# Spreading the sample tokens' rows over all partitions: DRAM scratch in place of selector matmuls

## The chip, the core and the metric

One core of a Trainium2 chip runs the whole program. The metric is the device time in microseconds (us), the median of several runs; less is better. The engines that matter are TensorE (PE, matmuls and transposes, with its weight loads shown apart as PEld), VectorE (DVE), ScalarE (ACT), GpSimd (POOL), and SyncE (SP), which here does nothing but issue the DMAs, one after another in program order.

## What is computed

One layer of a hybrid decoder runs for 256 prompt tokens and for 8 sample tokens, one each of 8 sequences. Two pieces of it treat the sample tokens apart, because each of the 8 has a state or a cache of its own. Everything else is large projections over 264 token columns.

```python
# retention, per head: every sample token b has its own 128 x 128 state
new_state = state * chunk_decay + k^T v        # rank-one update of that token's state
out       = q . new_state
# cross-attention, per head of 512 channels: every sample token has its own 256 memory keys and values
s = einsum('bshd,bmhd->bhsm', q, mk) * 512 ** -0.5
p = softmax(s)
o = einsum('bhsm,bmhd->bshd', p, mv)
```

The outputs are the hidden rows of both groups, the memory keys and values of the prompt, the retention states of both groups, and one set of value rows of the sample tokens.

## The kernel before, in words

**The weight stream.** All projections are one stream of 524 chunks, a chunk being 256 x 512 weights in fp32 (512 KB). SP loads a chunk (`emit_dma`, L1024), ACT rounds it to fp32r (`wh`, L1030), DVE takes the remainder (`wl`, L1038), and PE multiplies: 24 matmuls, three per 128 x 128 piece (L152 to L154), each over 264 columns. A loop at L1066 walks through the chunks. For chunk i it emits the remainder `wl` of chunk i + 2, the DMA of chunk i + 6, and then the 24 matmuls of chunk i, in four points of six. There are 5 raw buffers and 4 for the split halves, so each engine can run only some chunks ahead of PE. Every engine executes its own instructions strictly in the order in which they were emitted.

**Deferred work.** At each of the four points of a chunk `run_point` (L210) advances the small work: every due chain, and then one step of the first due task. A task is a Python generator; `yield 5` means: go on in five points at the earliest. So the small work is laid between the weight matmuls, and its place is decided by counting points, not by time. `flush` (L228) advances the point counter with no weight matmul in between until no chain, task or store is left.

**Retention of the sample tokens** (L568, eight heads, chunks 24 to about 75). The k and q columns of a head's 8 sample tokens are transposed to rows (L584), split into two fp32r halves in the tile `kq` (rows 0 to 7 and 32 to 39), and for each token b a matmul with a selector column of `sel`, broadcast to 128 columns, puts the sum of the two halves of row b on all 128 partitions, in the PSUM tile `bc` (L618). DVE then updates that token's state (L621) and multiplies it with the q row (L624, the sum lands in `rs_t`). Two tokens make one step, and a step is followed by `yield 2`.

**Cross-attention of the sample tokens** (`sample_attn`, L806, four heads in one lane, one after another). The q columns are transposed in four pieces (L810), split into `qs`, and for each token one selector matmul over 512 columns puts its q row on all partitions (`qb`, L819). DVE multiplies it with the token's keys (`kjk`, L822); the keys and later the values come as tiles `kv` of 512 KB with three buffers (`kv_fill`, L748, L752). The 16 columns of scores are transposed (L828), `softmax` (L790) works on 8 rows of 256, the probabilities are split into `pst`, and a selector matmul over 256 columns per token puts them on all partitions (`pb`, L842). DVE multiplies them with the values in four pieces per token (`vjk`, L845). At the end `join_o` (L785) writes the 8 sample columns of the head's output pair `oh`, `ol` next to the prompt's 256.

**Where the order ties these together.** The projection w_co starts at chunk 224 (`n_mem`) and reads the pairs `oh`, `ol` of head 0 in its chunks 224 and 225, of head 1 in 226 and 227, of head 2 in 228 and 229, and of head 3 from chunk 230 on. At chunk 230 (L1080) the loop calls `flush`, so that all work of the cross-attention is emitted ahead of the matmuls of chunk 230.

Of the kernel before, what the change touches and what calls it, by code (L numbers as in the profile page):

```python
# [30 lines left out]
def build(tc, I, O):  # L31
# [5 lines left out]
    with cst as cst, wpool as wpool, spool as spool, tpool as tpool, psum as psum:  # L37
        with tc.manual_schedule():
            _emit(tc, cst, wpool, spool, tpool, psum, I, O)


def _emit(tc, cst, wpool, spool, tpool, psum, I, O):
# [41 lines left out]
    sel = cst.tile([128, 8], F32R, name="sel")  # L84
# [115 lines left out]
    def store(dst, src, delay=10):  # L200
        stores.append((now[0] + delay, dst, src))
# [8 lines left out]
    def run_point():  # L210
# [13 lines left out]
        while stores and stores[0][0] <= now[0]:  # L224
            _, dst, src = stores.popleft()
            sp.dma_start(out=dst, in_=src)
# [131 lines left out]
    def clear():  # L358
        zt = half("zt")
        dve.memset(zt[:], 0.0)  # L360
        S["kq"] = [S["rpool"].tile([128, 256], F32R, name="kq", tag="kq", bufs=2) for _ in range(2)]
        yield
        for i in range(2):
            act.copy(S["kq"][i][:], zt[:, 0:256])
        dve.tensor_tensor(out=sel[:], in0=ident[:, 0:8], in1=ident[:, 32:40], op=ALU.add)
        act.activation(halfgn[:], gcol[:, G_GN:G_GN + 8], AF.Copy, scale=0.5)
# [179 lines left out]
    def ev_v(g):  # L546
        def ev(ps):
# [4 lines left out]
            if g == 0:  # L552
                S["state"] = {}
                load_state(0)
                load_state(1)
            for h in range(4 * g, 4 * g + 4):
                defer(retention(h), 3 + 16 * (h % 2), lane=f"r{h % 2}")
# [9 lines left out]

    def retention(h):  # L568
# [9 lines left out]
        kq = S["kq"][h % 2]  # L578
        tp = misc([128, 512], "tp")
# [3 lines left out]
        for i, src in enumerate((kt, qt)):  # L583
            transpose(tp[0:8, 256 + i * 128:384 + i * 128], src[:, 0:8])  # L584
# [3 lines left out]
        act.copy(kq[0:8, :], tp[0:8, 256:512])  # L588
        dve.tensor_tensor(out=kq[32:40, :], in0=tp[0:8, 256:512], in1=kq[0:8, :].bitcast(F32), op=ALU.subtract)
# [22 lines left out]
        yield  # L612
        rs_t = S["rpool"].tile([128, 8], F32, name="rs_t", tag="rs_t", bufs=2)
        for b0 in range(0, 8, 2):
            bc = misc([128, 2, 256], "bc")
            for j in range(2):
                b = b0 + j
                pe.matmul(bc[:, j, :], lhsT=sel[:, b:b + 1].broadcast_to([128, 128]), rhs=kq[:], start=True, stop=True)  # L618
            for j in range(2):
# [3 lines left out]
                j2 = S["rpool"].tile([128, 128], F32, name="rjk", tag="rjk", bufs=1)  # L623
                dve.scalar_tensor_tensor(out=j2[:], in0=st[:, b, :], scalar=1.0, in1=bc[:, j, 128:256],  # L624
                                         op0=ALU.mult, op1=ALU.mult, accum_out=rs_t[:, b:b + 1])
            yield 2
# [129 lines left out]
    def ev_cq(h):  # L756
        def ev(ps):
            if h == 0:
                zt = half("zt")
                dve.memset(zt[:], 0.0)  # L760
                S["qs"] = S["mpool"].tile([128, 512], F32R, name="qs", tag="qs", bufs=1)
                S["pst"] = S["mpool"].tile([128, 256], F32R, name="pst", tag="pst", bufs=1)
                act.copy(S["qs"][:], zt[:])
                act.copy(S["pst"][:], zt[:, 0:256])
# [40 lines left out]

    def sample_attn(h):  # L806
# [403 lines left out]
```

## Time and profile before

| | before |
|---|---|
| time, median of 3 runs | 1607.97 us (1607.68 to 1608.06) |
| span of the profiled execution, first to last instruction | 1605.7 us |
| time of the runs less that span | 2.3 us |
| PE busy | 1589.0 us, 99% |
| PE weight loads busy | 1560.8 us, 97% |
| DVE busy | 1049.4 us, 65% |
| ACT busy | 743.9 us, 46% |
| all DMA queues together | 326.15 MB, mean 203 GB/s |
| mean granted TensorE clock | 0.997 |

The page gives no time of the profiled execution other than its span. A busy PE row overlaps: matmuls are pipelined and a record of 284 ns starts about 120 ns after the one before it, so what a matmul costs PE is read from the distance between starts and not from its duration. Times of transfers are given from issue to landing.

### The profile page before, as it was taken

Reading aid. Unit: us, or ns where it says so; the run is one execution under the profiler, and the core shown is the slowest. Engines: PE = TensorE matmul, PEld = TensorE weight load, DVE = VectorE, ACT = ScalarE, POOL = GpSimd, SP = SyncE. Lnnn points to the kernel's source line nnn. Section 1 sums busy time; section 2 is a strip of 40 time slices with the busy share of each in tenths; the row PEclk is TensorE's granted clock in tenths of the full one; section 3 lists DMA queues with packets and bytes.
Section 4 is the critical chain, followed back from the end, with each engine's and each line's share of the span. In section 5 each row is a group of like instructions: output and inputs, shape, how many; then the busy total and the mean of one; then the engine's idle time right before and its main releaser. Section 6 shows DMA issues by size and latency. Waiting matters only on the chain.

```text
span 1605.7 us, 31031 instructions
## 1 busy us (share of the span) xinstructions
PE 1589.0 (99%) x12608; PEld 1560.8 (97%) x12608; DVE 1049.4 (65%) x1897; ACT 743.9 (46%) x1156; POOL 146.5 (9%) x138
## 2 busy tenths in 40 slices
PE   8999999999999999999999999999999999999997
PEld 7999999999999998999999999999999999999997
DVE  8758688678668777877655554554655555565555
ACT  5445466357444444444545443534444353444432
POOL 7403022010012111001000000000000000000000
PEclk9999999999999999999999999999999999999999
DMA  7565655455578887877555555455555555555552
GB/s 262 184 224 197 218 175 194 143 189 208 192 250 284 311 311 284 275 277 255 177 184 175 180 171 196 172 182 186 172 186 171 195 172 186 182 180 187 172 185 80
DMA packets 94222, 326.15 MB, mean 203 GB/s; under 512 B 10608, under 2 KB 15344, under 8 KB 94080
## 3 DMA queue, kind: packets, MB, share of 16 engines
q1 hardware_dynamic: 94080, 324.18, 59.2%
q8 instruction: 98, 1.61, 0.4%
q14 instruction: 44, 0.36, 0.1%
HBM read 313.03 MB, written 11.11 MB: 202 GB/s over the span
## 4 chain that ended last, share of the span: by engine, by line
PE 96%; DVE 2%; DMA 0%; issue 0%; ACT 0%; SPq 0%; POOL 0%; DVEq 0%; ACTq 0%
PE acc L152 28%; PE acc L153 28%; PE acc L154 28%; PE acc L176 2%; PE acc L178 2%; PE acc L177 2%; PE tp L96 1%; DVE wl L1038 1%; PE qb L819 0%; DMA hT<-in_xT_dram 0%; PE bc L618 0%; DVE xl L104 0%; PE spp L482 0%; DVE y L1121 0%; PE rsb L290 0%
## 5 line engine op out<-in xcount | busy, mean ns | idle before, releaser
L1030 ACT CAST wh<-w 128x1024 fp32r<-128x1024 f32 (+1 forms) x513 | 536.3, 1046 | 721.6 <-PE acc L153 638.7
L1038 DVE TENSOR_TENSOR wl<-w,wh 128x1024 fp32r<-128x1024 f32 (+1 forms) x513 | 631.2, 1243 | 255.1 <-ACT wh L1030 254.4
L152 PE MATMUL acc<-h2h,wh 128*128 128x264 f32 x1024 | 291.1, 284 | 0.0
L153 PE MATMUL acc<-h2l,wh 128*128 128x264 f32 x1024 | 291.0, 284 | 0.0
L154 PE MATMUL acc<-h2h,wl 128*128 128x264 f32 x1024 | 290.9, 284 | 0.0
L153 PE MATMUL acc<-rl,wh 128*128 128x264 f32 x992 | 282.3, 285 | 0.0
L154 PE MATMUL acc<-rh,wl 128*128 128x264 f32 x992 | 282.1, 284 | 0.0
L152 PE MATMUL acc<-rh,wh 128*128 128x264 f32 x992 | 282.1, 284 | 0.0
L152 PE MATMUL acc<-xh,wh 128*128 128x264 f32 x768 | 225.4, 293 | 0.2
L154 PE MATMUL acc<-xh,wl 128*128 128x264 f32 x768 | 219.9, 286 | 3.5 <-DVE wl L1038 2.9
L153 PE MATMUL acc<-xl,wh 128*128 128x264 f32 x768 | 219.6, 286 | 0.0
L152 PEld LDWEIGHTS acc<-h2h,wh 128*128 128x128 f32 x1024 | 192.9, 188 | 0.0
L153 PEld LDWEIGHTS acc<-h2l,wh 128*128 128x128 f32 x1024 | 192.8, 188 | 0.0
L154 PEld LDWEIGHTS acc<-h2h,wl 128*128 128x128 f32 x1024 | 192.6, 188 | 0.0
L152 PEld LDWEIGHTS acc<-rh,wh 128*128 128x128 f32 x992 | 187.0, 189 | 0.0
L153 PEld LDWEIGHTS acc<-rl,wh 128*128 128x128 f32 x992 | 186.8, 188 | 0.0
L154 PEld LDWEIGHTS acc<-rh,wl 128*128 128x128 f32 x992 | 186.5, 188 | 0.0
L154 PEld LDWEIGHTS acc<-xh,wl 128*128 128x128 f32 x768 | 145.7, 190 | 4.4 <-DVE wl L1038 3.7
L152 PEld LDWEIGHTS acc<-xh,wh 128*128 128x128 f32 x768 | 145.7, 190 | 1.9 <-ACT xh L103 0.7
L153 PEld LDWEIGHTS acc<-xl,wh 128*128 128x128 f32 x768 | 145.8, 190 | 0.2 <-DVE xl L104 0.2
L950 DVE TENSOR_TENSOR hT<-hT,acc 128x264 f32<-128x264 f32 x124 | 53.3, 430 | 73.4 <-PE acc L154 73.4
L92 POOL TENSOR_TENSOR msr<-msv,neghalf 128x3 f32<-128x3 f32 (+1 forms) x5 | 7.8, 1551 | 944.9 <-DVE msv L265 738.6
(255 smaller groups left out, 2800.0 us busy)
## 6 DMA issues: line engine op xcount, KB each, us to landing
w<-in_w_ff_dram SPq DMA_DIRECT2D x256, 512.0 KB, 4.1
w<-in_w_in_dram SPq DMA_DIRECT2D x95, 512.0 KB, 3.9
w<-in_w_out_dram SPq DMA_DIRECT2D x32, 512.0 KB, 4.1
w<-in_w_cq_dram SPq DMA_DIRECT2D x32, 512.0 KB, 4.2
kv<-in_kN_dram SPq DMA_DIRECT2D x32, 512.0 KB, 4.9
kv<-in_vT_dram SPq DMA_DIRECT2D x32, 512.0 KB, 5.2
w<-in_w_ck_dram SPq DMA_DIRECT2D x32, 512.0 KB, 5.3
w<-in_w_cv_dram SPq DMA_DIRECT2D x32, 512.0 KB, 4.4
```

The costliest lines, as they stand in the source:

```text
L92: gp.tensor_tensor(out=out, in0=in_, in1=neghalf[0:in_.shape[0], 0:n], op=ALU.pow)
L96: pe.transpose(out, in_, ident[0:p, 0:p])
L152: pe.matmul(ps, lhsT=a, rhs=xh, start=(i == 0), stop=False)
L153: pe.matmul(ps, lhsT=a, rhs=xl, start=False, stop=False)
L154: pe.matmul(ps, lhsT=b, rhs=xh, start=False, stop=(i == nk - 1))
L176: pe.matmul(ps, lhsT=a, rhs=hi[:, k, :], start=(kt == 0), stop=False)
L177: pe.matmul(ps, lhsT=a, rhs=lo[:, k, :], start=False, stop=False)
L178: pe.matmul(ps, lhsT=b, rhs=hi[:, k, :], start=False, stop=(kt == 15))
L950: dve.tensor_tensor(out=h[m], in0=h[m], in1=ps[m][:], op=ALU.add)
L1030: act.copy(hi[:, k, :], raws[i][:, k, :])
L1038: dve.tensor_tensor(out=lo[:, k, :], in0=raw[:, k, :], in1=hi[:, k, :].bitcast(F32), op=ALU.subtract)
```

## The change

The selector `sel`, the zeroed tiles `kq`, `qs` and `pst` and every matmul with `sel` are gone. Rows reach the partitions through DRAM instead: a small tile of rows is stored to a DRAM tile of the new pool `dpool`, and a DMA reads one row (or two) back with the same source for all 128 partitions.

- Retention: a new task `sample_rows(g)` gathers the k and q columns of four heads, transposes them in two pieces, copies them to a tile of 32 rows and stores it. Each step of two tokens reads its rows as a tile `bkq` of 128 x 512 (four buffers, asked for one step ahead). A step is followed by `yield 4` instead of `yield 2`, and the steps wait until the store has been emitted, then 6 points more.
- Cross-attention: the q columns are transposed in one piece and stored as `qd`; each token's row comes back as a tile `brow` of 128 x 512 (three buffers, two tokens ahead). The probabilities are stored as `pd` and come back as 128 x 256. Between the stages stand new waits of some points: 8, until the store was emitted, and 4 for the q rows; until the store was emitted, 4, and 4 for the probabilities.
- Stores are emitted when their own due time has come, no longer strictly first in, first out.

```diff
     def store(dst, src, delay=10):
-        stores.append((now[0] + delay, dst, src))
+        e = [now[0] + delay, dst, src, False]
+        stores.append(e)
+        return e
...
+    def sample_rows(g):
+        cols = S["rpool"].tile([128, 2, 32], F32, name="kqcol", tag="kqcol", bufs=1)
+        for i, w in enumerate("kq"):
+            act.copy(cols[:, i, :].rearrange("p (m b) -> p m b", m=4), S[w][g][:, :, 0:8])
+        yield 2
+        tp = misc([32, 2, 128], "tp")
+        for i in range(2):
+            transpose(tp[:, i, :], cols[:, i, :])
+        rows = S["rpool"].tile([32, 256], F32, name="kqrow", tag="kqrow", bufs=1)
+        act.copy(rows[:], tp[:].rearrange("p a d -> p (a d)"))
+        S["kqd"][g] = dpool.tile([32, 256], F32, name=f"kqd{g}")
+        S["kqe"][g] = store(S["kqd"][g][:], rows[:], 3)
+        yield
+
+    def rows_of(h, b0):
+        t = S["rpool"].tile([128, 2, 256], F32, name="bkq", tag="bkq", bufs=4)
+        r = 8 * (h % 4) + b0
+        sp.dma_start(out=t[:].rearrange("p b f -> p (b f)"),
+                     in_=S["kqd"][h // 4][r:r + 2, :].rearrange("b f -> (b f)").partition_broadcast(128))
+        return t
...
         for b0 in range(0, 8, 2):
-            bc = misc([128, 2, 256], "bc")
-            for j in range(2):
-                b = b0 + j
-                pe.matmul(bc[:, j, :], lhsT=sel[:, b:b + 1].broadcast_to([128, 128]), rhs=kq[:], start=True, stop=True)
+            bc = ahead
+            if b0 < 6:
+                ahead = rows_of(h, b0 + 2)
...
-            yield 2
+            yield 4
...
+    def spread_row(src):
+        t = S["mpool"].tile([128, 512], F32, name="brow", tag="brow", bufs=3)
+        n = src.shape[-1]
+        sp.dma_start(out=t[:, 0:n], in_=src.partition_broadcast(128))
+        return t
...
+        sc = small(16, "scs")
+        yield 8
+        while not e[3]:
+            yield 1
+        rows = deque(spread_row(qd[b].rearrange("m d -> (m d)")) for b in range(2))
+        yield 4
...
+            sent.append(store(pd[:], p[0:8, :], 2))
+            yield
+
+        sent = []
         softmax(tp[:], 8, spread_p)
         yield 11
+        while not sent or not sent[0][3]:
+            yield 1
+        yield 4
+        rows = deque(spread_row(pd[b]) for b in range(2))
+        yield 4
```

The order of the instructions moves with it. The first place is DVE around the values of head 3, the last head of the cross-attention. In the program before, its last groups of four products `vjk` stand between the remainders `wl` of the weight chunks, and `ol<-so` is the write of the head's sample columns:

```order
L793 TENSOR_SCALAR nb<-mx 128x1
L845 SCALAR_TENSOR_TENSOR vjk,so<-kv,pb 128x256 x4
L798 RECIPROCAL rc<-sm 128x1
L799 TENSOR_SCALAR ex<-ex,rc 128x256
L792 TENSOR_REDUCE mx<-sc 128x1
L793 TENSOR_SCALAR nb<-mx 128x1
L1038 TENSOR_TENSOR wl<-w,wh 128x1024
L798 RECIPROCAL rc<-sm 128x1
L799 TENSOR_SCALAR ex<-ex,rc 128x256
L1038 TENSOR_TENSOR wl<-w,wh 128x1024
L908 TENSOR_TENSOR pl<-tp,ph 128x256 x2
L101 TENSOR_TENSOR ol<-so,oh 128x4x8
```

In the changed program the same place on DVE reads as follows; `mx` to `ex` with 8 rows is the softmax of the sample tokens:

```order
L843 SCALAR_TENSOR_TENSOR kjk,scs<-kv,brow 128x512 x2
L1065 TENSOR_TENSOR wl<-w,wh 128x1024
L101 TENSOR_TENSOR ol<-op,oh 128x256 x2
L1065 TENSOR_TENSOR wl<-w,wh 128x1024
L801 TENSOR_REDUCE mx<-tp 8x1
L802 TENSOR_SCALAR nb<-mx 8x1
L807 RECIPROCAL rc<-sm 8x1
L808 TENSOR_SCALAR ex<-ex,rc 8x256
L872 SCALAR_TENSOR_TENSOR vjk,so<-kv,brow 128x256 x32
L101 TENSOR_TENSOR ol<-so,oh 128x4x8
L1065 TENSOR_TENSOR wl<-w,wh 128x1024 x2
```

All 32 products of head 3 now stand in one piece behind its softmax, with no remainder of a weight chunk among them. The second place is SP at the same point. Before, the last loads of values and the weight chunks of w_co take turns:

```order
L752 DMA kv<-in_vT_dram 128x1024
L1024 DMA w<-in_w_co_dram 128x1024
L752 DMA kv<-in_vT_dram 128x1024
L1024 DMA w<-in_w_co_dram 128x1024 x4
L226 DMA out_mem_v_dram<-vnat 128x1024
L1024 DMA w<-in_w_co_dram 128x1024 x23
```

In the changed program SP has, from the third load of values of head 3 on (`pd_8989` is the DRAM tile of head 3's probabilities):

```order
L767 DMA kv<-in_vT_dram 128x1024
L227 DMA pd_8989<-ex 8x256
L818 DMA brow<-pd_8989 128x256 x3
L767 DMA kv<-in_vT_dram 128x1024
L818 DMA brow<-pd_8989 128x256
```

The pair of one `kv` and one `brow` comes five times in all, then the weight chunks of w_co follow. So the store of the probabilities, the eight loads of their rows and five of the eight loads of values now stand together, where a load of values and a load of weights took turns.

The third place is PE where it transposes the score columns of head 3 (`tp<-cmat,scs`). Before, that stands in chunk 214, in the projection to the memory's keys and values:

```order
L153 MATMUL acc<-meml,wh 128x256
L154 MATMUL acc<-memh,wl 128x256
L96 MATMUL tp<-cmat,scs 8x128 x2
L152 MATMUL acc<-memh,wh 128x256
L153 MATMUL acc<-meml,wh 128x256
```

In the changed program it stands in the middle of chunk 229, in w_co:

```order
L153 MATMUL acc<-ol,wh 128x264
L154 MATMUL acc<-oh,wl 128x264
L96 MATMUL tp<-cmat,scs 8x128 x2
L152 MATMUL acc<-oh,wh 128x264
L153 MATMUL acc<-ol,wh 128x264
```

Twelve matmuls of chunk 229 follow it, and then chunk 230, the first that reads the pair of head 3. The transposes have moved 15 chunks towards the end; those of heads 0, 1 and 2 moved from chunks 147, 169 and 191 to 149, 175 and 202.

More of the change, by code (lines that the diff above doesn't have):

```diff
@@ L83, in _emit @@
     neghalf = cst.tile([128, 4], F32, name="neghalf")
-    sel = cst.tile([128, 8], F32R, name="sel")
     w00 = cst.tile([8, 8], F32, name="w00")
@@ L223, in run_point @@
                 break
-        while stores and stores[0][0] <= now[0]:
-            _, dst, src = stores.popleft()
-            sp.dma_start(out=dst, in_=src)
+        for e in [e for e in stores if e[0] <= now[0]]:
+            sp.dma_start(out=e[1], in_=e[2])
+            e[3] = True
+            stores.remove(e)
     def flush():
@@ L758, in ev @@
             if h == 0:
[L759 to L764, printed above, removed]
                 kv_fill()
@@ L804, in softmax @@
         return ex
-    def sample_attn(h):
-        qs, pst = S["qs"], S["pst"]
-        tp = misc([8, 512], "tp")
-        for m in R4:
-            transpose(tp[:, m * 128:(m + 1) * 128], q8[h][:, m, :])
-        act.copy(qs[0:8, :], tp[:])
-        dve.tensor_tensor(out=qs[32:40, :], in0=tp[:], in1=qs[0:8, :].bitcast(F32), op=ALU.subtract)
-        sc = small(16, "scs")
-        yield
+    def spread_row(src):
[3 more added lines that the diff above has]
+        return t
+    def sample_attn(h):
+        tp = misc([32, 128], "tp")
+        transpose(tp[:], q8[h][:].rearrange("p m b -> p (m b)"))
+        q32 = half("q32")[0:32, 0:128]
+        act.copy(q32, tp[:])
+        qd = dpool.tile([8, 4, 128], F32, name=f"qd{h}")
+        pd = dpool.tile([8, 256], F32, name=f"pd{h}")
+        e = store(qd[:].rearrange("b m d -> m b d"), q32, 3)
+        sc = small(16, "scs")
+        yield 8
[3 more added lines that the diff above has]
+        yield 4
         for b in range(8):
@@ L817, in sample_attn @@
             kc = kvq.popleft()
-            qb = misc([128, 512], "qb")
-            pe.matmul(qb[:], lhsT=sel[:, b:b + 1].broadcast_to([128, 128]), rhs=qs[:], start=True, stop=True)
+            if b < 6:
+                rows.append(spread_row(qd[b + 2].rearrange("m d -> (m d)")))
+            qb = rows.popleft()
             for i in range(2):
@@ L840, in sample_attn @@
             vc = kvq.popleft()
-            pb = misc([128, 256], "pb")
-            pe.matmul(pb[:], lhsT=sel[:, b:b + 1].broadcast_to([128, 128]), rhs=pst[:], start=True, stop=True)
+            if b < 6:
+                rows.append(spread_row(pd[b + 2]))
+            pb = rows.popleft()
             for d in R4:
                 jk = half("vjk")
-                dve.scalar_tensor_tensor(out=jk[:, 0:256], in0=vc[:, d * 256:(d + 1) * 256], scalar=1.0, in1=pb[:],
-                                         op0=ALU.mult, op1=ALU.mult, accum_out=so[:, d, b:b + 1])
+                dve.scalar_tensor_tensor(out=jk[:, 0:256], in0=vc[:, d * 256:(d + 1) * 256], scalar=1.0,
+                                         in1=pb[:, 0:256], op0=ALU.mult, op1=ALU.mult, accum_out=so[:, d, b:b + 1])
             yield 4
```

34 lines of the change are left out of this document (12 added, 22 removed).

## The prediction

> **What bounds the kernel now.** I read the page first: its busy times, and the chain that ended last.
>
> ```profile
> span 1605.7 us, 31031 instructions
> PE 1589.0 (99%) x12608; PEld 1560.8 (97%) x12608; DVE 1049.4 (65%) x1897; ACT 743.9 (46%) x1156; POOL 146.5 (9%) x138
> PE 96%; DVE 2%; DMA 0%; issue 0%; ACT 0%; SPq 0%; POOL 0%; DVEq 0%; ACTq 0%
> ```
>
> TensorE is the bound from end to end: 96% of the chain are matmuls, and DVE, with 65%, appears for 2%. So a matmul removed is worth the time it holds PE, provided that whatever takes its place never lets PE wait. I then asked for the busy time by stretches, and for who waited for the rows that are to change.
>
> ```profile
> 10.00:17.00 7.00, 4.06 (x28) 3.63 (x29) 7.00 (x8) 6.56 (x13) 6.69 (x8) 0.98 1.03 417
> 17.00:24.00 7.00, 7.00 (x48) 7.00 (x47) 7.00 (x7) 2.49 (x4) 6.76 (x8) 0.77 0.84 290
> ...
> 520.00:750.00 230.00, 230.00 (x1549) 211.40 (x1548) 181.10 (x472) 102.75 (x155) 30.98 (x24) 1.00 0.83 292
> ...
> DVE kjk L822 <- PE qb L819: 20.1, 19, 1.5
> ...
> DVE vjk L845 <- PE pb L842: 9.6, 20, 2.3
> ```
>
> The columns of a stretch are its length, the busy time of PE, PEld, DVE, ACT and POOL, the granted clock, the DMA share and GB/s. In the cross-attention (520 to 750 us) PE never rests, DVE is busy for 181 of 230 us, and the DMA engines for 0.83 of the time at 292 GB/s, against 417 GB/s in the stretch that opens the kernel. DVE waits 29.7 us for the selector matmuls, but those waits are off the chain.
>
> **What the change removes from PE.** What an instruction costs is the distance from its start to the next start in the timeline of PE (start, duration, engine, line, operation).
>
> ```profile
> 99.03 0.40 PE L618 MATMUL bc<-kq,sel 128*128 128x256 f32 x2
> 99.26 0.28 PE L152 MATMUL acc<-xh,wh 128*128 128x264 f32 x1
> ...
> 465.93 0.39 PE L819 MATMUL qb<-qs,sel 128*128 128x512 f32 x1
> 466.16 0.28 PE L152 MATMUL acc<-h1h,wh 128*128 128x264 f32 x1
> ...
> 505.19 0.28 PE L842 MATMUL pb<-pst,sel 128*128 128x256 f32 x1
> 505.31 0.28 PE L152 MATMUL acc<-h1h,wh 128*128 128x264 f32 x1
> ...
> 530.42 0.44 PE tp L96 x4
> ```
>
> The first line holds two `bc` matmuls in 0.23 us; there are 8 heads x 8 tokens = 64, so 7.4 us. One `qb` takes 0.23 us; 32 of them 7.4 us. One `pb` takes 0.12 us; 32 of them 3.8 us. The last row, from the chain, has four transposes in 0.44 us. Sixteen small ones go from the cross-attention and sixteen from retention; four come in each. That is 24 fewer at 0.11 us, 2.6 us. Together 21.2 us; with the rounding of the start times, 20.5 to 21.8. The splits of `kq`, `qs` and `pst` on ACT and DVE go too, and the constants; they are worth nothing, since both engines idle beside a busy PE.
>
> **What it adds where there is cover.** 32 reads of `bkq` and 32 of `brow` with 256 KB each and 32 of 128 KB are 21 MB on SP's queue, and ten small stores. In the cross-attention it is 12.6 MB in about 290 us, some 43 GB/s on top of 292, still below the 417 that the opening stretch reached. A `brow` is asked for two tokens, ten points, ahead of its use. A chunk has four points and 24 matmuls at 0.12 us, 2.9 us, so that is 7.2 us. A `bkq` is asked for one step, four points or 2.9 us, ahead, and SP runs about one chunk ahead of DVE, because its weight loads wait only for a `wl` that stands a chunk earlier.
>
> ```profile
> L752 SPq DMA_DIRECT2D kv<-in_kN_dram x32: 327/328/1469, 454.4 to 698.6; - x32
> ...
> DMA to landing us min/median/max: 3.3/5.0/7.0
> L226 SPq DMA_DIRECT2D out_state_p_dram<-so x8: 383/424/592, 102.3 to 249.4; - x8
> ...
> DMA to landing us min/median/max: 3.1/3.2/4.0
> L1124 SPq DMA_DIRECT2D out_yT_dram<-y x9: 332/393/418, 1597.4 to 1601.8; - x9
> ...
> DMA to landing us min/median/max: 1.7/2.3/2.8
> ```
>
> The 512 KB of a `kv` tile land in 5.0 us at the median, so 256 KB come in about 5 us or less, inside 5.8 and 7.2 us. Queued on SP behind a read that must wait for its store are the next weight loads, with a lead of six chunks. I put 1 us on all of this: 0 if every row is in time (no gain is possible, since PE has no idle time there), 5 if the rows of the 32 retention steps come late and DVE's slack of two chunks doesn't hold them.
>
> **What it adds where there is none.** The new waits and the wider spacing stretch each head's lane, and the order shows the end of it: the transposes of head 3's scores stand in the middle of chunk 229, and all 32 products `vjk` are emitted by the `flush` at chunk 230. The matmuls of chunk 230 read the pair that `join_o` completes behind those products. Twelve matmuls remain as cover; then PE must wait. I work out the chain from the start of the transposes, with the same operations in the program before (timeline around head 0's softmax, a later group of values, and head 3's join):
>
> ```profile
> 496.96 0.38 PE L96 MATMUL tp<-cmat,scs 128*8 128x128 f32 x2
> 497.38 0.41 DVE L792 TENSOR_REDUCE mx<-tp 8x1 f32<-8x256 f32 x1 [1.41 <-PE tp L96]
> 498.06 0.47 ACT L795 ACTIVATE ex<-tp,nb 8x256 f32<-8x256 f32 x1 [2.15 <-PE acc L154]
> 498.43 0.18 ACT L795 ACTIVATION_READ_ACCUMULATOR ex<-tp,nb 8x1 f32 x1
> 499.05 0.14 DVE L798 RECIPROCAL rc<-sm 8x1 f32<-8x1 f32 x1
> 499.22 0.34 DVE L799 TENSOR_SCALAR ex<-ex,rc 8x256 f32<-8x256 f32 x1
> ...
> 741.64 0.42 DVE L845 SCALAR_TENSOR_TENSOR vjk<-kv,pb 128x256 f32<-128x256 f32 x1 [0.32 <-PE pb L842]
> ...
> 743.01 1.22 DVE L1038 TENSOR_TENSOR wl<-w,wh 128x1024 fp32r<-128x1024 f32 x1
> ...
> 754.27 0.23 ACT L100 CAST oh<-so 128x32 fp32r<-128x32 f32 x1
> ...
> 755.09 0.18 DVE L101 TENSOR_TENSOR ol<-so,oh 128x32 fp32r<-128x32 f32 x1
> ```
>
> - Softmax: from 496.96 to the end of the sum at 498.61 is 1.65 us; reciprocal and scaling take 0.51. That is 2.2 us. The order puts a `wl` (1.2 us) ahead of the row maximum that also waits for ACT; I add 0.4, with bounds of 0 and 1.2.
> - The store of 8 KB and then the first row of 128 KB, each to landing and one after the other, since the read needs what the store wrote. No such pair is in the trace. The nearest rows are the stores of y at the quiet end (1.7 at least, 132 KB) and of the states beside weight traffic (3.2 at the median, 64 KB). The queue here is nearly quiet, so I take 2.0 and 2.3, with bounds of 1.7 and 3.3 each (3.3 being the fastest `kv`, four times as large), and 0.2 for two wake-ups. First products at 2.6 + 4.5 = 7.1 us.
> - The products: four per token, 743.01 less 741.64, 1.37 us. Three `kv` and three `brow` tiles are there at the start. Token 3 needs the buffer of token 0, so its loads are issued only when token 0 is done, and they come L later; tokens 6 and 7 go round once more. The last product ends after 4 x 1.37 + 2 L. L is the landing of a `kv` and the issue of the `brow` behind it (0.4 us): 3.7 us by the fastest `kv`, 5.4 by the median one; I take 4.0, near the fastest, because no weight load runs beside it. That is 13.5 us, 12.9 to 16.3.
> - The join: 0.23 and 0.18 us with two hand-overs, 0.7 us.
>
> Sum: 21.3 us after the transposes began. PE has those two (0.2) and twelve matmuls (1.5) to do, so it idles for 19.6 us. From both ends of the bounds: 17.3 to 25.3.
>
> Then the clock. In the stretch from 10 to 17 us PE was busy for 4.06 of 7 us, and in the next one the granted clock is 0.77: 0.23 x 7 = 1.6 us of full-speed work were lost after a pause of about 3 us. A pause of 20 us must cost at least that; I take 2.0, with a bound of twice the row, 3.2. [...]
>
> **The sum.** Against the span: 1605.7 - 21.2 + 19.6 + 2.0 + 1.0 = 1607.1 us. The runs' median lies 2.3 us above the span, so 1609.4 us, 0.1% above before. A gain of 1.3% on PE is spent on one wait of about the same size. A measurement of this kernel can tell about 0.2%, 3.2 us, from no change; inside are 1604.8 to 1611.2 us.
>
> **The rivals.** *The wait is no wait* (the pair is ready in time, by an overlap that I miss): the full gain less the 1 us of the rows, 1587.8 us. For it speaks that DVE idles for a third of the kernel; against it the order, with 32 products between softmax and join and nothing but twelve matmuls beside them. 4%. A milder form has every transfer at its lowest price: 17.3 + 1.6 + 0 - 21.8 = -2.9, 1605.1 us; only with a cheaper L still would it be faster by over 0.2%.
>
> *The transfers keep their loaded prices in the gap* (slower). SP works in order, so the loads of tokens 3 to 7 go out in pairs, each pair behind a wait for DVE. If a pair lands like the median `kv` among traffic, L is 5.4, and with store and row at 3.2 us each the first products start at 9.2. The idle time is then 9.2 + 16.3 + 0.7 - 1.7 = 24.5, and with 2.6 for the clock the result is 1605.7 - 21.2 + 24.5 + 2.6 + 1.0 + 2.3 = 1614.9 us. It decides from the point where wait, clock and late rows together pass 24.4 us, as by an L of 4.9. For it: the median over 64 loads is 5.0, and the waits here are a chain without slack. Against it: the store and the y rows land in 2 us when the queue is quiet. 27%.
>
> *Rows come late all along the stage* (slower): if `bkq` or `brow` take a loaded 7 us, as the slowest `kv`, retention's steps run behind the lead of 5.8 us, DVE's remainders `wl` come late and PE waits at some of 32 steps. With 1.2 us at a quarter of them, 10 us more: 1619 us. Against it is DVE's idle time, 49 of 230 us in the dense stage. 9%.
>
> **How the numbers follow.** The forecast, 1609.4 us, has 60% with its own range of 1605 to 1614; the loaded transfers 27%, late rows 9%, no wait 4%. Faster by over 0.2% are the last case and a small part of the forecast's, 0.10. Slower by over 0.2% are the loaded transfers for the most part, the late rows, and the upper end of the forecast's own range: 0.42. Within 0.2% remains 0.48. The range of 8 in 10 leaves out the case without a wait and most of the late rows: 1603.8 to 1617 us.
>
> **What would show it.** In the changed profile PE should lack the rows `bc`, `qb` and `pb`, its instructions should be about 150 fewer (128 matmuls and 24 transposes), and six chunks into w_co there should be one gap of some 20 us ahead of a matmul `acc<-oh,wh`, released by ACT or DVE at the join, with the 32 products inside it in three rounds of three, three and two, and a granted clock below 1 just behind. Inside it, `pd` and the first `brow` should take about 4.3 us together. DVE should show waits for `brow` in that gap and hardly any elsewhere; PE's idle time outside should stay as before. I am wrong if the gap is under 15 or over 27 us, if PE idles at many small places instead, or if the removed matmuls are worth less than 20 us.

## The result, and the profile after

The changed kernel takes 1618.9 us (median of four runs, 1616.0 to 1620.3) against 1608.0 us of the kernel before in the same session: slower by a factor of 1.0066, with a 95% interval of 1.0053 to 1.0079. The forecast of 1609.4 us and its range of 1603.8 to 1617.0 were too low. The profiled execution is the longest of the four (1620.3 us).

These rows of the page answer to those of before.

```profile
span 1618.5 us, 30800 instructions
PE 1572.3 (97%) x12456; PEld 1545.0 (95%) x12456; DVE 1055.5 (65%) x1878; ACT 738.3 (46%) x1146; POOL 154.5 (10%) x138
PE 88%; DMA 5%; DVE 4%; issue 1%; POOL 0%; SPq 0%; ACT 0%; DVEq 0%; ACTq 0%
```

PE has 152 instructions fewer, as forecast, and 16.7 us less busy time although some of it ran at half speed. On the chain PE fell from 96% to 88%, and DMA and DVE, 2% together before, now hold 9%. PE's waits say for what (who, for whom, us in total, times, longest):

```profile
PE acc L152 <- ACT oh L100: 22.5, 1, 22.5
PE tp L96 <- DVE kjk L843: 3.3, 3, 2.6
...
PE rp L96 <- DVE va L451: 1.7, 1, 1.7
PE tp L96 <- DVE ex L808: 1.3, 1, 1.3
...
PE acc L152 <- DVE ra L528: 1.2, 2, 0.6
```

One wait of 22.5 us stands ahead of a matmul `acc<-oh,wh`, released by ACT at the join. Beside it there are several waits of 0.6 to 2.6 us. Summed from the gaps in its timeline between 85 and 790 us, PE idles for 30.1 us; before it was 0.4 us over the same stretch.

The chain of waits shows what the long gap is made of (start, us, what; rows under 0.1 us are left out).

```profile
753.84 0.23 PE tp L96 x2
754.10 0.42 DVE mx L801
...
754.78 0.57 ACT ex L804 x2
...
755.92 1.29 DMA pd<-ex
757.28 2.88 DMA brow<-pd
760.18 0.53 DVE vjk L872 x3
...
764.45 0.33 SPq L767
764.83 5.51 DMA brow<-pd
...
770.36 0.33 SPq L767
...
770.74 5.35 DMA brow<-pd
...
776.22 1.48 DVE vjk L872 x8
...
777.72 0.23 ACT oh L100
```

Softmax, the store of `pd` in 1.29 us, the first row in 2.88 us, then the products, and twice a pair of loads (`SPq` issues the `kv`) whose row lands 5.5 and 5.4 us after it was asked for: this is the chain of the prediction, link by link. The first products begin 6.5 us after the score transposes (753.68 in PE's timeline; 7.1 forecast). The last ends 17.5 us after that (13.5 forecast).

The clock is read from stretches of PE (length, PE busy, granted clock, DMA share, GB/s).

```profile
573.00:576.00 3.00, 2.35 (x11) 0.51 1.02 411
...
778.00:781.50 3.50, 3.50 (x17) 0.54 0.32 103
781.50:785.00 3.50, 3.50 (x31) 1.00 0.63 201
```

After the long gap PE does 17 matmuls in 3.5 us and then 31 in the next 3.5: 14 matmuls of 0.12 us, 1.7 us, are lost. The row from 573 us shows a second spell at half speed, behind a gap of only 2.65 us. PE is busy for 2.80 us of it, so it costs about 1.4.

So the account is: 1605.7 - 21.2 (removed) + 22.5 (the gap) + 7.2 (the other gaps, 30.1 less 22.5 and 0.4) + 3.1 (clock) = 1617.3 of the 1618.5 us measured. About 1 us of the rest lies in how gaps are read: a record of 284 ns outlasts the 0.12 us to the next start by 0.16 us and hides that much of each gap, and there are six gaps more than before. The other gaps were the surprise. Here is the largest of them, in the timeline around 570 us.

```profile
567.39 0.69 DVE L843 SCALAR_TENSOR_TENSOR kjk<-kv,brow 128x512 f32<-128x512 f32 x1 [1.93 <-DMA brow<-qd]
...
568.65 1.05 ACT L1057 CAST wh<-w 128x1024 fp32r<-128x1024 f32 x1 [3.60 <-DMA w<-in_w_ck_dram]
...
572.66 0.69 DVE L843 SCALAR_TENSOR_TENSOR kjk<-kv,brow 128x512 f32<-128x512 f32 x1 [2.83 <-DMA brow<-qd]
...
573.42 0.38 PE L96 MATMUL tp<-cmat,scs 128*8 128x128 f32 x1 [2.65 <-DVE kjk L843]
```

A q row comes late, DVE stands still for it, and PE cannot pass the score transposes that need the last product, though weight matmuls wait behind them. A weight chunk lands late at the same place. The transfers say why (from issue to landing; first all `brow`, then all `kv`):

```profile
DMA to landing us min/median/max: 2.9/5.2/9.0
...
DMA to landing us min/median/max: 3.3/6.1/8.9
```

The trace has the landing of 16 of the 64 rows: some take up to 9.0 us where the forecast counted on 5 and a lead of 7.2. `kv` went from a median of 5.0 (46 landings of 64) to 6.1 (17). Two stretches around the gap (length, busy PE, PEld, DVE, ACT, POOL, clock, DMA share, GB/s):

```profile
555.00:565.00 10.00, 10.00 (x46) 8.16 (x45) 8.52 (x17) 3.35 (x4) 0.00 (x0) 1.00 0.99 372
565.00:575.00 10.00, 7.12 (x31) 5.38 (x30) 5.25 (x11) 3.31 (x5) 0.00 (x0) 0.90 0.96 378
```

The DMA engines are full there, at 372 to 378 GB/s.

### The profile page after: what moved, and what is told of

Its sections match the earlier page's. It is cut to its first block, busy times and chain, and to the rows that moved or that the text cites. A ratio compares the mean times of both kernels' runs of the same rounds, so it can differ in the third digit from the quotient of the medians.

```text
span 1618.5 us, 30800 instructions
## 1 busy us (share of the span) xinstructions
PE 1572.3 (97%) x12456; PEld 1545.0 (95%) x12456; DVE 1055.5 (65%) x1878; ACT 738.3 (46%) x1146; POOL 154.5 (10%) x138
## 4 chain that ended last, share of the span: by engine, by line
PE 88%; DMA 5%; DVE 4%; issue 1%; POOL 0%; SPq 0%; ACT 0%; DVEq 0%; ACTq 0%
PE acc L152 27%; PE acc L153 27%; PE acc L154 27%; DVE wl L1065 1%; DMA brow<-pd 1%; DMA brow<-qd 1%; PE acc L177 1%; PE acc L178 1%; PE acc L176 1%; DMA qd<-q 1%; PE tp L96 1%; DVE vjk L872 1%; DMA w<-in_w_ck_dram 1%; DVE kjk L843 0%; DMA hT<-in_xT_dram 0%
```

## The experiments

Four theories stand in the expectations. A: the one wait at the flush is the whole loss. B: the rows' traffic slows all transfers. C: SP, in order, waits for the stores of the rows. D: the rows are asked for too late, so DVE, in order, waits for them. All ratios are to the kernel before, with 95% intervals; idle times of PE are summed from its timeline between 85 and 790 us (800 where a lane moved).

**The lane made tighter,** so that head 3 ends ahead of the flush (keys first, then values):

```diff
-            yield 5
+            yield 4
-            yield 4
+            yield 3
```

> The changed kernel with two waits shortened: a step over the keys is followed by 4 points in place of 5, a step over the values by 3 in place of 4, so that the products of head 3 end at chunk 226 and no longer in the flush at chunk 230. Theory A (one wait: the gap of 22.5 us at chunk 230 and the half clock behind it, 1.6 us, are the larger part of what the change adds, and the crowded cross-attention is the smaller part, 4.6 us of idle time and 1.6 us of clock): the gap is gone and the rest stays, so about 1618.9 - 24 = 1595 us, with PE's idle time in the cross-attention at 4 to 8 us. Theory B (the transfers: the row reads crowd the DMA engines, and the gap is only where the lateness is collected): the same bytes now come in fewer points, rows and weights come later, and PE idles 15 us or more in the cross-attention at many places; 1603 to 1612 us.

It took 1613.14 us, 1.0039 (1.0024 to 1.0054), above what either theory allowed. The long gap is gone and only 6 of its 24 us came back. In the profiled execution, with 1617.8 us the longest of the four, PE now idles 21.2 us, at 19 places, and three spells at half speed cost it about 7 us more.

```profile
PE acc L154 <- DVE wl L1065: 6.8, 3, 3.5
PE tp L96 <- DVE ex L808: 5.6, 3, 3.1
PE tp L96 <- DVE kjk L843: 5.3, 4, 2.5
```

Weight remainders (3.6 of the 6.8 us in the lane, the rest at the start of the kernel), softmax and scores are late in turn, all on DVE. A is not the whole story.

**The two halves of the change apart:** retention through DRAM with the old cross-attention, and the reverse. The edit swaps whole functions; its heart in the first run is

```diff
-            qb = rows.popleft()
+            qb = misc([128, 512], "qb")
+            pe.matmul(qb[:], lhsT=sel[:, b:b + 1].broadcast_to([128, 128]), rhs=qs[:], start=True, stop=True)
```

and in the second the same for `bc` in retention.

> Only the retention part of the change; the cross-attention keeps its selector matmuls. PE loses 64 matmuls of 0.115 us and twelve transposes net, 8.7 us. The changed kernel's trace shows 3.1 us of new idle time before 300 us. Theory A and theory B both see no gap and no crowded stage here: 1608.0 - 8.7 + 3 = 1602 us. If the retention stage has a hidden price as well (GpSimd and VectorE slow each other, seen as state updates of 0.88 us in place of 0.35), it is nearer to 1606.

> Only the cross-attention part of the change; retention keeps its selector matmuls. The gain is 12.6 us (64 matmuls and twelve transposes). Theory A: the gap with its clock, 24 us, the crowded stage with its clock, 6 us: 1608.0 - 12.6 + 30 = 1625 us, so that this part alone makes the whole loss. Theory B expects the same sum but with no single gap over 15 us if the traffic of retention was not what filled the queues before it. If both parts carry the loss evenly: 1613 us.

Retention alone is faster: 1601.64 us, 0.9961 (0.9947 to 0.9975), with 3.1 us of idle time (0.6, 0.6, 1.7, 0.2). The cross-attention alone is slower, about as A expected: 1626.89 us, 1.0120 (1.0104 to 1.0137), with the one long gap.

```profile
PE acc L153 <- ACT oh L101: 22.6, 1, 22.6
```

**The traffic alone:** the kernel before, with reads that nobody uses, ahead of each `qb` (and likewise 128 x 256 ahead of each `pb`):

```diff
+            spread_row(I["kN"][h, b][0, 0:512])
             qb = misc([128, 512], "qb")
```

> The kernel before with its selector matmuls, and beside them one read per token of 128 x 512 (keys) or 128 x 256 (values) elements from the caches, the same source for all partitions, into a tile that nobody reads: 64 more reads, 12.6 MB, at the places where the changed kernel asks for its rows. Nothing waits for them but the next such read into the same buffer. Output as before. Theory A: PE's slack covers the traffic, 1608 to 1610 us. Theory B: the traffic alone makes weights late and PE idle, 1614 us or more.

1607.91 us, 1.0000 (0.9991 to 1.0009), PE idle 0.4 us, with the engines as full as after the change:

```profile
515.00:535.00 20.00, 20.00 (x166) 19.87 (x165) 16.35 (x53) 7.01 (x8) 1.59 (x2) 1.00 1.00 375
555.00:575.00 20.00, 20.00 (x105) 16.88 (x105) 15.39 (x35) 9.44 (x14) 4.38 (x4) 1.00 1.01 372
```

In the old lane 12.6 MB more cost nothing as long as no engine waits for them. B, by itself, falls there.

**No read waits for a store:** the tight lane with rows taken from the caches.

```diff
-        rows = deque(spread_row(qd[b].rearrange("m d -> (m d)")) for b in range(2))
+        rows = deque(spread_row(I["kN"][h, b][0, 0:512]) for b in range(2))
```

> The kernel of e1, but the rows of the cross-attention are read from the caches (same sizes, same places in the order, same waits of VectorE for them), so that no read has to wait for a store; the stores of q and p stay. Output: the scores and the sample tokens' attention are computed with other numbers. e1 idles 21 us on TensorE and e4, where nobody waits for the same reads, 0.4 us. Theory C (the store: SyncE stops at the first read of a phase until the store has landed, and weights, keys and rows queue behind it): the idle time of the cross-attention goes, 18 us to under 4, and the time is near 1596 us. Theory D (the lead: VectorE reaches the product before its row has landed, because two tokens are too short a lead when a read takes 6 us): little changes, 1609 to 1614 us.

**Three tokens ahead:** the tight lane, `brow` with four buffers, rows asked for three tokens ahead, keys and values alike.

```diff
-            if b < 6:
-                rows.append(spread_row(pd[b + 2]))
+            if b < 5:
+                rows.append(spread_row(pd[b + 3]))
```

> The kernel of e1 with the rows of the cross-attention asked for three tokens ahead in place of two (four buffers). Theory D (lead too short): VectorE's waits for rows and with them most of the 18 us of TensorE's idle time go, 1597 to 1600 us. Theory C (the store's landing holds SyncE's queue): the first rows of a phase are no earlier, so at most a third goes, 1608 to 1614 us.

**The row reads on GpSimd's queue:** the tight lane, with rows two tokens ahead.

```diff
-        sp.dma_start(out=t[:, 0:n], in_=src.partition_broadcast(128))
+        gp.dma_start(out=t[:, 0:n], in_=src.partition_broadcast(128))
```

> The kernel of e1 with the row reads of the cross-attention issued by GpSimd; the stores and all else stay on SyncE. SyncE then never waits for a store to land. Theory C: weights and keys are no longer late behind a row read, and most of the 18 us goes, about 1598 us, unless GpSimd's own work, which stands in the same order, is held up by the reads in its turn. Theory D: the rows are as late as before and VectorE still waits in front of the next weight remainder, 1609 to 1614 us.

With no read waiting for a store: 1612.17 us, 1.0025 (1.0015 to 1.0035), 1 us less than the tight lane, and the two intervals overlap. DVE waits 31.5 us for rows there and 29.9 in the tight lane, so C is small. From GpSimd: 1618.99 us, 1.0071 (1.0056 to 1.0086), worse than either theory allowed. GpSimd's own work stands in one order with these reads, and it waits 49.5 and 47.2 us for `brow` buffers; that this is the reason was not shown. Three ahead: 1605.99 us, 0.9988 (0.9979 to 0.9997), 7 us less, between the readings of D and C. DVE's waits, three ahead:

```profile
DVE kjk L843 <- issue: 14.6, 5, 7.6
...
DVE kjk L843 <- DMA brow<-qd: 2.6, 2, 1.3
DVE vjk L872 <- DMA brow<-pd: 2.5, 2, 2.0
```

and in the tight lane with two ahead (the times behind the last bar are idle time and what ended it):

```profile
L872 DVE SCALAR_TENSOR_TENSOR vjk<-kv,brow 128x256 f32<-128x256 f32 x128 | 52.4, 466 | 15.7 <-DMA brow<-pd 15.5
L843 DVE SCALAR_TENSOR_TENSOR kjk<-kv,brow 128x512 f32<-128x512 f32 x64 | 49.1, 803 | 24.1 <-DMA brow<-qd 14.4 <-issue 9.7
```

The waits for rows fall from 29.9 to 5.1 us, with 6.8 us for `kv` beside them, while the idle time for which the profile shows no releaser grows from 9.7 to 14.6. Of this, 10.4 us stand ahead of the first products of heads 1 and 3, whose row is still asked for only four points ahead (`yield 4` was kept). D is part of it; 14.2 us of idle time remain on PE. Both runs that ask three ahead also give `so` two buffers in place of four.

**Another order of the lane:** q rows stored as soon as they are there, the keys of head h + 1 ahead of the values of head h, rows up to three ahead across the borders.

```diff
+    phases = [("k", 0), ("k", 1), ("v", 0), ("k", 2), ("v", 1), ("k", 3), ("v", 2), ("v", 3)]
```

> The changed kernel with the cross-attention's lane in another order: the q rows of every head are stored as soon as they exist, the keys of head h + 1 are worked on ahead of the values of head h, and rows are asked for up to three tiles ahead across these borders, no sooner than four points after their store was emitted. Steps keep 5 and 4 points; the lane ends at chunk 215. Whatever the cause, store or lead, both are covered here: no gap, TensorE idle under 6 us in all, 1608 - 21.3 + 4 = 1591 us. If the loss comes from elsewhere (for one, products with both operands in SBUF that slow down beside GpSimd), idle time of 10 us or more stays: 1598 us or more.

1608.34 us, 1.0003 (0.9993 to 1.0012), idle 13.9 us: no better than three ahead. The rows were not covered: DVE still waits 24.0 us for them. Two of its products also take 2.9 us in place of 0.7 beside GpSimd (below).

**Tight lane and traffic, with the selectors,** and then **the tight lane with nothing else:** the kernel before with the unread reads and the edit of the tight lane, and with that edit alone.

> The kernel before (selector matmuls, nothing waits for a stored row) with the 64 unread row reads of the traffic run and with the tight lane: 4 points per token for keys and 3 for values. It asks whether the 21 us of idle time in the tight-lane run came from the tight lane itself (kv tiles asked for 25% faster) or from waiting for the rows. If from the rows (my theory): PE idles under 3 us in the cross-attention and the time stays within 0.3% of before, 1605 to 1612 us. If from the tight lane: PE idles 10 us or more at many places, 1618 us or more.

> The kernel before with the tight lane alone (4 points per key token, 3 per value token), no row reads. The traffic with the tight lane cost 11.5 us (1619.5) and the same traffic with the old lane nothing (1607.9). Two readings. Rate: what counts is how many bytes a step asks for; the weights' 512 KB per chunk of 2.9 us and a kv tile of 512 KB per token make 362 GB/s here for keys, with the traffic 452, and the transfers reached 372 to 405 at a share of 1.0. Then this run keeps within 4 us of before, 1606 to 1612. Lane: the denser work on DVE and ACT alone delays the weights' halves, whatever the traffic. Then 1616 us or more.

With the reads 1619.5 us, 1.0073 (1.0058 to 1.0088), against my theory. Without them 1613.25 us, 1.0042 (1.0026 to 1.0059), between the two readings. The spacing of the lane is a cost of its own, 5 us; the reads add 6 us in the tight lane and 0 in the old one. The rates in this and the later expectations (362, 452, 399 and 407 GB/s) take 2.9 us for a chunk. In this stage a chunk takes 3.25 us (before, 64 chunks from 534.6 to 742.8 us), which makes them 323, 403, 355 and 363. One caveat: in the run with the reads SP itself stands in line for the two buffers of the unread rows (8.8 us for those of the keys in the old lane).

```profile
SPq L809 <- DMA brow<-in_kN_dram: 27.7, 19, 2.5
```

So part of the 6 us may be SP's order, not bandwidth. And of the 11.5 us by which that span grew, gaps (6.3, and 0.4 before) and clock (1.7) explain 7.6, and a later start 1.2 (the first matmul `acc<-h1h`, ahead of the lane, comes at 436.6 us, before at 435.4). The rest lies within PE's busy time, where gaps under 0.16 us do not show, and stays open.

**The row's place alone:** the kernel before; ACT copies each row from PSUM to SBUF, and DVE reads the copy.

```diff
+            act.copy(brow[:], qb[:])
+            qb = brow
```

> The kernel before; ACT copies each broadcast row from PSUM to SBUF and the products read the copy. No DMA is added. It measures by itself what a product costs whose tensor operands both lie in SBUF. If they collide with GpSimd there (my theory): the slowest kjk takes over 1.0 us and the mean rises from 0.685 to 0.70 or more, only while GpSimd works, as after the change; if the slow products after the change came from the DMA that writes rows into SBUF, all kjk stay at 0.67 to 0.69 us. Time: within 0.3% of before in both, since DVE has slack, 1606 to 1612 us.

1613.86 us, 1.0037 (1.0024 to 1.0050), a little more than either reading allowed. ACT, in order, now waits for the selector matmuls as well (28.8 and 12.7 us), which is a likely reason and was not tested. The durations of the key products (ns, min/median/max) in the kernel before:

```profile
L822 DVE SCALAR_TENSOR_TENSOR kjk<-kv,qb x64: 676/683/690, 466.4 to 713.2; 128x512 f32<-128x512 f32 x64
```

after the change:

```profile
L843 DVE SCALAR_TENSOR_TENSOR kjk<-kv,brow x64: 676/688/1239, 464.5 to 748.7; 128x512 f32<-128x512 f32 x64
```

and with the copy:

```profile
L825 DVE SCALAR_TENSOR_TENSOR kjk<-kv,brow x64: 675/691/1255, 466.7 to 719.0; 128x512 f32<-128x512 f32 x64
```

With the copy, all 8 key products that overlap GpSimd's work take 0.97 to 1.25 us and the other 56 0.68 to 0.69; before, 12 overlap it and all take 0.68 to 0.69. No row is read by DMA in the copy run, so the slow products do not come from such reads.

With 4 points per key token the collision reaches PE. There it meets the last key product ahead of the score transposes of head 2 (the run with only the queries through DRAM, below):

```profile
629.44 2.79 POOL L910 TENSOR_TENSOR vl<-vnat,vh 128x1024 fp32r<-128x1024 f32 x1 [18.97 <-ACT vh L908]
...
629.96 2.82 DVE L849 SCALAR_TENSOR_TENSOR kjk<-kv,brow 128x512 f32<-128x512 f32 x1
...
632.84 0.27 PE L97 MATMUL tp<-cmat,scs 128*8 128x128 f32 x1 [2.47 <-DVE kjk L849]
```

The product ends 0.55 us behind GpSimd's instruction, and PE stands still for 2.47 us; where that product takes 0.69 us, as three ahead, it is 0.34. The same 2.82 and 2.47 us stand in the tight lane, with no read waiting for a store, with the rows from GpSimd's queue and with half rows. None of the four theories has this, so about 2 us of what each of these runs idles is neither bytes nor lead.

**Only a part of the cross-attention through DRAM,** with retention: first the probabilities (`pb` is a row read, `qb` a selector matmul), then the queries (the reverse), both with 4 points per key token; then the queries with 5 points for heads 0 and 1. Below, the first piece belongs to the first run, the second to the other two, the last to the third.

```diff
-            qb = rows.popleft()
+            qb = misc([128, 512], "qb")
...
-            pb = rows.popleft()
+            pb = misc([128, 256], "pb")
...
-            yield 4
+            yield 5 if h < 2 else 4
```

> Retention's rows and the probabilities through DRAM, the queries of the cross-attention by selector matmuls as before, 4 points per key token, so that head 3 is done ahead of chunk 230. Against the retention-only run (1601.64 us) PE loses 32 pb matmuls, 3.8 us, and the row reads are 128 KB instead of 256. If the late q rows (256 KB, 6.4 us to landing) are what idles PE: 4 us or less of idle time in the cross-attention, 1597 to 1602 us. If any wait of DVE for a DRAM row costs as much as it saves: 1602 to 1608 us.

> Retention's rows and the queries of the cross-attention through DRAM, the probabilities by selector matmuls as before, 4 points per key token, so that head 3 is done ahead of chunk 230. Against the retention-only run (1601.64 us) PE loses 32 qb matmuls and some transposes, 9 us. If the late q rows are what idles PE: 10 us or more of idle time in the cross-attention, 1601 to 1610 us; if the lane's second wait (the store of the probabilities and its rows) carries it: 1594 to 1600 us.

> As the run with only retention's rows and the queries through DRAM (1599.18 us), with 5 points per key token for heads 0 and 1 and 4 for heads 2 and 3. By the rate theory heads 0 and 1 then ask for 399 GB/s instead of 452 in their key phases, and PE idles less in the first half of the cross-attention: 1595 to 1599 us. If the spacing plays no part: 1599 to 1601; above 1603 only if head 3 is now late at chunk 230.

Probabilities: 1603.46 us, 0.9972 (0.9960 to 0.9984), idle 5.3 us in the profiled execution, the fastest of six; no gain over retention alone. Queries: 1599.18 us, 0.9949 (0.9933 to 0.9966), idle 7.0 us. Both are the second reading. Eased: 1598.33 us, 0.9939 (0.9924 to 0.9953), idle 6.5 us; the two overlap, so the easing is not shown to help. That version is the fastest of this study. DVE still waits for its rows there:

```profile
DVE kjk L849 <- DMA brow<-qd: 20.0, 8, 4.3
```

but PE has only one longer gap in the cross-attention, 2.7 us behind a softmax, with a spell at half speed behind it, and with nothing to store between softmax and values head 3 is done in time.

**Half the bytes, the same waits:** the tight lane, reading half of each row (the keys' rows are shown; the probabilities' likewise).

```diff
-        sp.dma_start(out=t[:, 0:n], in_=src.partition_broadcast(128))
+        if n == 512:
+            sp.dma_start(out=t[:, 0:256], in_=src[0:256].partition_broadcast(128))
+            return t[:, 0:256].unsqueeze(1).broadcast_to([128, 2, 256])
```

> The changed kernel with the tight lane (1613.14 us), but only the first half of each row of the cross-attention is read, and the products use it twice (the sample tokens' attention has other values). DVE does the same work with the same waits; the rows' bytes are halved, from 8.4 and 4.2 MB. By the rate theory the demand in the key phases falls from 452 to 407 GB/s, the rows land earlier, and about half of the 21 us of idle time goes: 1600 to 1607 us. If the wait for each row is a matter of its round trip and not of bytes, the time stays: 1611 to 1615 us.

**Three ahead in the old lane:** the changed kernel with 5 and 4 points, and this edit for keys and values:

```diff
-        t = S["mpool"].tile([128, 512], F32, name="brow", tag="brow", bufs=3)
+        t = S["mpool"].tile([128, 512], F32, name="brow", tag="brow", bufs=4)
...
-                rows.append(spread_row(qd[b + 2].rearrange("m d -> (m d)")))
+                rows.append(spread_row(qd[b + 3].rearrange("m d -> (m d)")))
```

> The changed kernel with its own lane (5 and 4 points), rows asked for three tokens ahead instead of two. The wait of 22.5 us at the flush stays (20 to 24). It asks what the 7 us of idle time outside it are made of: if a lead of two tokens was too short, they fall to 3 us, retention's, and the one half-speed spell outside the gap goes, 1613 to 1616 us; if the lead plays no part, 1617 to 1620 us.

Half rows: 1608.81 us, 1.0009 (0.9999 to 1.0019), 4.3 us less than the tight lane, with 13.9 us of idle time: just outside what either reading gave, so bytes count, but not for everything. DVE's waits for rows hardly fall, from 29.9 to 27.3 us. Three ahead in the old lane: 1614.57 us, 1.0041 (1.0026 to 1.0056), 4.3 us less than the change itself.

```profile
PE acc L152 <- ACT oh L100: 21.6, 1, 21.6
...
PE tp L96 <- DVE kjk L843: 1.5, 3, 0.8
```

The long gap stays, the gap of 2.65 us shrinks to 0.8, and the half-speed spell behind it is gone. That shows D in the changed kernel itself, at this place.

## Why the prediction was wrong

**The removed matmuls: right.** 128 matmuls and 24 transposes for 21.2 us. In retention alone 64 `bc` and 12 transposes, 8.7 us by the forecast's prices, went; the span fell by 5.9 and PE idled 2.7 us more, together 8.6.

**The wait at the flush: right in place and mechanism, 2.9 us too small.** 22.5 us against 19.6, inside the bounds of 17.3 to 25.3 (their own terms, with the wake-ups, add up to 17.7 and 25.5). Store and first row cost 4.3 us (4.5 forecast). The loads behind them were mis-sized: L was taken as 4.0 us "because no weight load runs beside it". Counted as there, from the issue of a pair until its row is there, it was 5.8 and 5.9 us: by the timeline the pair of token 4 is issued at 763.06 when the products of token 1 are done, its own products begin at 768.87 and end at 770.34, and then the pair of token 7 goes out, whose products begin at 776.22. That is above the 5.4 of the second rival; its store and row at 3.2 each were too dear. Up to three pairs of loads were in flight at once, and a weight load from 771.22 on; that they slow one another is likely and was not tested. The quiet queue holds for the first row only.

**The clock: 2.0 us forecast, 1.7 behind the gap.** The unexpected second spell adds 1.4. No run shows the 2.6 us that the second rival took; behind the long gap it was 1.7. In the changed run's trace the granted clock is 0.50 from 573.03 to 576.44 us, behind the gap of 2.65 us, and from 760.77 to 781.24, within and behind the gap of 22.5 us; ahead of both spells and behind them it is 1.00. Here are the 3.41 us ahead of the first spell, with most of the gap of 2.65 us, and then two stretches as long, over which a gap of 2.47 us fell in the run with only the queries through DRAM (second number: PE busy; matmuls of 256 columns start 0.12 us apart behind that gap, where they start 0.21 us apart in the spell at 0.50):

```profile
569.62:573.03 3.41, 1.15 (x5) 0.57 (x4) 0.58 (x2) 2.29 (x4) 0.00 (x0) 1.00 1.03 412
...
627.95:631.36 3.41, 2.32 (x19) 1.93 (x17) 2.63 (x4) 1.41 (x2) 1.92 (x1) 1.00 1.03 407
631.36:634.78 3.42, 1.94 (x17) 1.94 (x18) 3.37 (x6) 0.30 (x1) 0.87 (x1) 1.00 0.99 371
```

PE stood still for 2.26 us of the first stretch and for 1.09 and 1.48 us of the other two. What decides whether such a gap is followed by half speed was not shown.

**The covered rows: the step that failed.** "I put 1 us on all of this", with 5 as the bound. It was 7.2 us of idle time and 1.4 of clock. Some 2.7 of the 7.2 are retention's; the longest gap there, 1.7 us, stands behind other work of DVE and no late row. 4.5 are the cross-attention's. DVE was to wait for rows "hardly any elsewhere" than in the long gap; 27 of its 37.5 us lie elsewhere. Here are these waits, then DVE at the first row of head 2 and SP at the last row of head 1, and a stretch of the kernel before:

```profile
DVE kjk L843 <- DMA brow<-qd: 22.7, 9, 4.8
...
DVE vjk L872 <- DMA brow<-pd: 14.8, 11, 4.3
...
632.92 0.69 DVE L843 SCALAR_TENSOR_TENSOR kjk<-kv,brow 128x512 f32<-128x512 f32 x1 [4.73 <-DMA brow<-qd]
...
564.82 0.64 SPq L818 DMA_DIRECT2D brow<-qd  x1
...
620.00:630.00 10.00, 10.00 (x45) 8.18 (x44) 7.81 (x16) 3.15 (x3) 0.00 (x0) 1.00 1.01 390
```

Three sentences of the working were wrong.

- "A `brow` is asked for two tokens, ten points, ahead of its use" does not hold for the first row of a head: between its request and its product the change has `yield 4`. DVE waited 1.2, 4.8, 4.7 and 2.8 us for the first q rows of the four heads, 13.5 of its 22.7 us. Behind the third (632.92) a softmax of the prompt stands in DVE's order, and PE idles 1.29 us for its `ex` at 636.8.
- "256 KB come in about 5 us or less": the last q row of head 1 was asked for at 564.82 and its product began at 572.66, 7.8 us later. DVE had been ready for it since 569.83, so its lead was 5.0 us and not 7.2. This is the gap of 2.65 us.
- "Some 43 GB/s on top of 292, still below the 417" averages over 290 us. The kernel before has full stretches already (1.01 at 390 GB/s). While a head's keys are read, a step of 5 points takes 4.1 us in this stage and asks for 512 KB of `kv` and 256 KB of row, beside the weights' 512 KB per 3.25 us: about 355 GB/s, and the engines gave 372 to 378. Where the average leaves 82 GB/s, this phase leaves about 20.

The third rival named late rows and a time of 1619 us. That its time was met is luck: it has 10 us at the steps of retention, and the runs show 8.6, most of it in the cross-attention, and 2.9 more at the flush. It was given 9% because DVE idles for 49 of 230 us, an average as well: where an engine works in order, idle time ahead of a late row is no reserve for what stands behind that row. Before, DVE waited nearly as long for the `qb` matmuls (20.1 us) at no loss, but never over 1.5 us at once; now one wait is up to 4.8.

**The likeliest result was thus a sum with the right main term.** Most of the miss came from a term that was priced from averages, and a part from L. What the runs show of the first one's cause: the lead (4.3 us in the old lane, 7 in the tight one), the bytes (4.3 us for half of them, tight lane), hardly the stores (1 us), and in the tight lane a collision with GpSimd (2 us of idle time). The traffic costs nothing in the old lane if nobody waits (1607.91). The tight lane itself costs 5 us. How these add up in the tight lane was not separated: 14 us of idle time remain three ahead, and which part of it is the first rows, which bandwidth, which GpSimd and which the order on DVE and SP stays open. Neither a first row asked for earlier, with all else kept, nor a lane longer than chunk 230, which would need no tightening, was tried.

## What to carry to other kernels

Price a transfer that an in-order engine waits for at the crowded stage's slowest landing; check the lead of the first one of a series by itself; and work out the demand of the phase in which it runs, not of the stage. Here 355 GB/s asked where 372 to 378 are given, and first rows with a lead of four points, made a covered term of 1 us into 8.6. Taking work off the busiest engine pays only where what replaces it is not in series with that engine: in retention, where a row has slack, the same exchange gained 6 us, and in the cross-attention it lost 19. Before a lane is stretched by waits, look at where its end must be, and when the end is tight, keep the step without a round trip (here the selector matmuls of the probabilities) in the last link.

## What the runs showed of the hardware

- A key product of DVE with both operands in SBUF took 0.97 to 1.25 us in place of 0.68 while GpSimd worked (the copy run: 8 of 8 that overlapped), and with one operand in PSUM 0.68 to 0.69 (before: all 12 that overlapped). Beside one long GpSimd instruction of 2.79 us one took 2.82. The prediction had not counted on it. GpSimd's work slowed 6 of the 64 `kjk` and 7 of the 128 `vjk` after the change, 3 and 4 us of DVE time; what that cost PE was not shown. In five runs with 4 points per key token one slow product held PE for 2.47 us.
- The DMA engines were at a share of 1.0 at 372 to 411 GB/s with one core at work. A row of 128 KB landed in 2.9 us when three rows were asked for with nothing else in the queue, and in 4.1 to 5.5 us when each followed a `kv` of 512 KB and up to three such pairs were in flight.
- A PE gap of 2.65 us was followed by 3.4 us at half speed, of which PE worked for 2.8, 1.4 us lost. In the other runs gaps near 2.5 us had such a spell behind them in some (traffic in the tight lane, 2.49 us from 641.9: matmuls of 256 columns then 0.21 us apart) and not in others (queries alone, 2.47 us from 630.4, and half rows, 2.48 us from 632.5: 0.12 us apart). The gap of 1.7 us at the end of retention had none in the changed run and in five others (interleaved phases, probabilities alone, queries alone and eased, half rows), with matmuls 0.12 us apart. So the length of a gap did not tell by itself what it cost: 2.65 us cost half its length and more once again, 2.47 us cost nothing more.
